# A folded Fourier layer: the end-token row moves from VectorE to TensorE, the weight splits become 1024 wide, and the modulation rows are handed out one per weight tile

## The chip, the cores and the metric

The kernel runs on one NeuronCore of one Trainium2 chip. The metric is the device time of one execution in microseconds; the figure for a kernel is the median of its timed runs. One further execution is taken by the hardware profiler, with a time of its own. The engines in the profile are PE (matmul), PEld (its weight load), DVE (VectorE), ACT (ScalarE) and SP, whose queue issues all the loads here; POOL is idle.

## The reference

Two layers over 256 latent tokens (`x`) and 256 context tokens (`ctx`) of width 2048, in float32. The even layer does retention (A) and Fourier mixing (B), the odd one a gated short convolution. Every layer is an adaLN-modulated RMSNorm first and a gated residual add last.

```python
shift, scale, gate = split(silu(c) @ ada_w[i] + ada_b[i], 3)      # per layer, also with c_ctx for ctx
hx = rmsnorm(x, norm_w[i]) * (1 + scale) + shift
# layer 0 (even): w_in is 2048 x 10240
qx, kx, vx, gax, ux, gbx = split(hx @ w_in);  qc, kc, vc, ... = split(hc @ w_in)
A = retention(qx, kx, vx | states of ctx) * silu(gax)
f = fft2(ux per group of 256 channels, over tokens and channels).real
B = (f @ fno_w per group) * silu(gbx)
x = x + gate * (concat(A, B) @ w_out)
# layer 1 (odd): w_in is 2048 x 16384
bg, cg, xt, g = split(h @ w_in);  y = bg * conv3(cg * xt) * silu(g)
x = x + gate * (y @ w_out)
return rmsnorm(x, final_norm_w)
```

The real part of the two-dimensional transform has a token symmetry: tokens t and 256-t enter only by their sum and their difference. So the kernel folds hx over the tokens (`fold_x`): 128 even columns (sums, t = 0..127) and 128 odd columns (differences). Column 0 of the sums holds tokens 0 and 128 added. Their difference goes in the place of the odd column 0, which has no use of its own there; it belongs to the even part of the channels. That is the end-token row, and it needs a projection of its own.

## The kernel before

**Splits.** Every weight tile is 128 x 2048 in float32, loaded by `load_raw` (line 83) from SP into a ring of three buffers, 1 MB each. `split_w` (line 88) cuts it into four pieces of 512 columns. Of each, ACT casts a rounded part `whi` (line 98) and DVE subtracts to get the rest `wlo` (`sub`, line 59). Both have rings of six. PE then multiplies `whi` by the activations, whose high and low parts lie side by side in 512 columns, and `wlo` by the high 256 columns alone. So one tile is 16 matmuls of 512 columns and 16 of 256 (`group_t`, line 123, PSUM tile `gT`). `group_n` (`gN`) does the same with the weights as the moving side, `group_d` (`gD`) in 256 columns. All matmuls have line 56.

**Order.** A scheduler that knows the program puts the instructions of each engine in a fixed order. Each engine then runs its own in that order and waits by semaphore. The program itself has two lists of side work. `hook()` takes one entry of `stages` after each half tile. `bg()`, called behind each tile's load, takes one of 64 `tasks`: a load of 1 MB of the modulation matrix (`raw<-adaT`, the same ring of three) and one pass of DVE over it (line 375, 128 x 2048). Row by row these make the gates of layer 0 and all the modulation of layer 1. While `quiet` is set, `bg()` does nothing; while `often` is set, it takes a task at every tile, and else at every second one. `finish_mods(first, last)` (line 762) does at once the rows below `last` that are still missing.

**Stages in time.** Prologue: modulation rows of layer 0 and the first projection, both bound to loads. Retention, four head pairs, with 28 tasks. In the last pair (quiet) `fold_x` makes the eight folded tiles `hf`, four of them during the queries' projection, three between heads, the last after the gates.

Then the Fourier part, still quiet: eight gate groups `gate_unfold` (line 724, two tiles each, from `hf`, the sigmoid's input unfolded by DVE), and beside the first four the 16 steps of `u0`, beside the last four the 16 steps of `u1` (class `half`, line 607). A step takes one 128-row block of the projection weights. `fold` adds and subtracts their halves on DVE (channels are folded too), two 512-wide splits follow, and six matmuls into `pu`. For the end-token row DVE also accumulates `uacc += weights * xd` (line 639), where `xd` is the end-token difference of hx; a matmul with `e0` puts the sum over partitions into row 0 of `pu` at the end. `u1`'s stages also run the Fourier matrices of groups 0 to 3 (`fourier`, line 660: `tables` with PSUM `pz`, `tokens` with `pP`, `product` with `py`, `gate`). Groups 4 to 7 run beside the first group of the output projection (`t_out`, line 757). `tables` loads its 256 KB (`wr`, line 675) itself. PSUM has three two-bank buffers (`pu`, `gT`, `gN`) and two one-bank buffers (all other names).

The output projection `w0o` (`project`, line 771) has eight blocks of four tiles. From block 6 on it is quiet. Line 756 has cleared `often`, so 12 tasks lie in its first six blocks. Behind it, `finish_mods(16, 48)` does eight rows in one go, then 16 `modulate` calls make `h1` for layer 1. Layer 1 is 16 blocks of eight tiles of `w1`, the first quiet, with the last 16 tasks behind it at every second tile; then eight blocks of `w1o`.

## Time and profile before

| | |
|---|---|
| three timed runs | 1850.09, 1849.87, 1865.33 us; median 1850.09 |
| the profiled execution | 1845.95 us, span 1844.1 us, mean granted PE clock 0.982 |
| PE / DVE / ACT busy | 1761.7 / 1271.0 / 895.6 us |
| loads | 397.03 MB read, 216 GB/s over the span |

A busy time counts an engine as busy while an instruction is in flight, and matmuls overlap, so a PE that shows as fully busy can still be slowed by its clock. The column PEclk tells that apart. The stages are read by a view that cuts the span into stretches and gives each engine's busy time in each, its clock and the loads' rate.

### The profile page before, as it was taken

The page shows a single profiled execution, that of the slowest core. Times are in us where ns is not written, and L with a number is a line of the kernel's source. Part 1 is how long each engine was busy: PE and PEld are TensorE (multiplying, and loading weights), DVE is VectorE, ACT ScalarE, POOL GpSimd, SP SyncE. Part 2 cuts the span into 40 slices and gives each one's busy share as a digit, 9 for nine tenths or more (in the row PEclk, how much of TensorE's full clock was granted, in tenths as well). Part 3 has the DMA queues.
Part 4 walks back from the last instruction along what each step waited for, and adds up shares of the span by engine and source line. Part 5 has one row for each costly group of instructions (what it writes and reads, how often), then busy time and mean ns, then how long its engine had stood idle before and what let it go on. Part 6 is the DMA issues. An engine that isn't in the chain of part 4 may idle for free.

```text
span 1844.1 us, 26501 instructions
## 1 busy us (share of the span) xinstructions
PE 1761.7 (96%) x10022; PEld 1506.7 (82%) x10022; DVE 1271.0 (69%) x2034; ACT 895.6 (49%) x1484; POOL 0.2 (0%) x4
## 2 busy tenths in 40 slices
PE   5999999999979997999969999999999999999997
PEld 3667888888858786888958888888888888888887
DVE  5448857756489996777687888666666666665554
ACT  4235625354445454445445555555555555555553
POOL 0000000000000000000000000000000000000000
PEclk9999999999989998999979999999999999999999
DMA  9886656652335554687666777555555555555552
GB/s 390 341 315 264 224 200 226 242 214 92 137 109 207 215 189 164 221 305 274 230 250 251 282 289 289 195 199 185 186 198 189 184 196 191 183 193 195 183 190 108
DMA packets 58737, 400.85 MB, mean 217 GB/s; under 512 B 6512, under 2 KB 6896, under 8 KB 11376
## 3 DMA queue, kind: packets, MB, share of 16 engines
q1 hardware_dynamic: 58608, 399.16, 59.2%
q8 instruction: 78, 1.28, 0.3%
q14 instruction: 51, 0.42, 0.1%
HBM read 397.03 MB, written 2.10 MB: 216 GB/s over the span
## 4 chain that ended last, share of the span: by engine, by line
PE 90%; DVE 4%; DMA 3%; ACT 1%; issue 1%; SPq 0%; DVEq 0%; ACTq 0%
PE gT L56 69%; PE gN L56 7%; PE gD L56 2%; PE gemv L56 2%; PE pu L56 2%; PE o L56 1%; DMA raw<-adaT 1%; PE pvx L56 1%; PE pk L56 1%; PE pvc L56 1%; DVE wlo L59 1%; DMA wr<-fno 1%; PE S L56 1%; PE pq L56 1%; DVE raw L375 1%
## 5 line engine op out<-in xcount | busy, mean ns | idle before, releaser
L59 DVE TENSOR_TENSOR wlo<-raw,whi 128x512 fp32r<-128x512 f32 x1056 | 714.7, 689 | 376.6 <-ACT whi L98 355.3
L98 ACT CAST whi<-raw 128x512 fp32r<-128x512 f32 x1024 | 626.8, 620 | 690.2 <-PE gT L56 512.1
L56 PE MATMUL gT<-h,whi 128*128 128x512 f32 x2048 | 712.6, 395 | 15.6 <-DVE h L202 15.0
L56 PE MATMUL gT<-h,wlo 128*128 128x256 f32 x2048 | 567.8, 278 | 0.0
L56 PEld LDWEIGHTS gT<-h,whi 128*128 128x128 f32 x2048 | 384.9, 188 | 105.4 <-issue 15.4
L56 PEld LDWEIGHTS gT<-h,wlo 128*128 128x128 f32 x2048 | 385.8, 188 | 0.4
L375 DVE CUSTOM_DVE_ANT_0 raw<-raw,scb 128x2048 f32<-128x2048 f32 x64 | 146.5, 2290 | 71.4 <-DMA raw<-adaT 68.2
L56 PE MATMUL gT<-hx,whi 128*128 128x512 f32 x448 | 161.6, 399 | 1.6 <-ACT v L493 1.6
L56 PE MATMUL gT<-y,whi 128*128 128x512 f32 x448 | 155.4, 394 | 0.0
L56 PE MATMUL gT<-hx,wlo 128*128 128x256 f32 x448 | 126.5, 282 | 0.0
L56 PE MATMUL gT<-y,wlo 128*128 128x256 f32 x448 | 124.1, 277 | 0.0
L56 PEld LDWEIGHTS gT<-hx,whi 128*128 128x128 f32 x448 | 83.9, 188 | 21.2 <-ACT v L493 2.1
L56 PEld LDWEIGHTS gT<-y,whi 128*128 128x128 f32 x448 | 84.0, 188 | 19.5
L56 PE MATMUL gT<-hf,whi 128*128 128x512 f32 x256 | 93.2, 400 | 1.7 <-ACT whi L98 1.7
L56 PEld LDWEIGHTS gT<-hx,wlo 128*128 128x128 f32 x448 | 84.6, 189 | 1.2 <-DVE wlo L59 0.5
L56 PEld LDWEIGHTS gT<-y,wlo 128*128 128x128 f32 x448 | 84.1, 188 | 0.0
L56 PE MATMUL gT<-yA,whi 128*128 128x512 f32 x224 | 80.4, 401 | 2.8 <-ACT whi L98 2.8
L56 PE MATMUL gT<-yB,whi 128*128 128x512 f32 x224 | 78.4, 394 | 0.2 <-ACT whi L98 0.2
L56 PE MATMUL gT<-hf,wlo 128*128 128x256 f32 x256 | 73.2, 286 | 0.3 <-DVE wlo L59 0.2
L185 ACT COPY lr_r<-gT 128x512 f32<-128x512 f32 x103 | 59.9, 581 | 7.3 <-PE gT L56 7.2
L56 PE MATMUL gT<-yA,wlo 128*128 128x256 f32 x224 | 63.0, 281 | 0.0
L56 PE MATMUL gT<-yB,wlo 128*128 128x256 f32 x224 | 62.1, 278 | 0.6 <-DVE wlo L59 0.6
(269 smaller groups left out, 2197.0 us busy)
## 6 DMA issues: line engine op xcount, KB each, us to landing
raw<-w SPq DMA_DIRECT2D x168, 1024.0 KB, 4.8
raw<-adaT SPq DMA_DIRECT2D x64, 1024.0 KB, 5.4
raw<-ada SPq DMA_DIRECT2D x32, 1024.0 KB, 7.0
raw<-w0o SPq DMA_DIRECT2D x32, 1024.0 KB, 4.9
raw<-w1o SPq DMA_DIRECT2D x32, 1024.0 KB, 4.8
raw<-w0g SPq DMA_DIRECT2D x16, 1024.0 KB, 4.8
raw<-w0u SPq DMA_DIRECT2D x16, 1024.0 KB, 4.8
raw<-w0s SPq DMA_DIRECT2D x8, 1024.0 KB, 5.7
```

What stands on the lines that cost most here:

```text
L56: nc.tensor.matmul(o, l, r, start=start, stop=stop, skip_group_check=True)
L59: nc.vector.tensor_tensor(o, x, hi.bitcast(F32), op=ALU.subtract)
L98: nc.scalar.copy(hi[:], sl)
L185: nc.scalar.copy(r[:], t[:, :, 256:512])
L375: nc.vector.tensor_tensor_reduce(out=raw[:], in0=raw[:], in1=scb[:], scale=1.0, scalar=0.0, op0=ALU.mult, op1=ALU.add, accum_out=gv[:, j:j ...
```

## The change

- **Splits 1024 wide.** `split_w` casts and subtracts 1024 columns at a time, with rings of three (the same memory). The first projection keeps 512 for the pieces that borrow other tiles.
- **End-token row on PE.** `xd` and `uacc` go. A tile `sd` holds the end-token column of `hf`, high and low, for each of the 16 blocks (`ends`). Each step adds two matmuls of 512 columns with 32 stationary columns into a bank `pd` that is held over the 16 steps. `finish` adds its two rows by a matmul with `e0` and copies them into row 0.
- **Steps.** A step folds its own 512 columns of weights (two DVE instructions of 512 instead of half of two of 1024) and splits sum and difference in one 1024-wide pair.
- **First gates from hx.** Gates 0 to 3 use the unfolded `hx`, with no unfolding after. Gates 4 to 7 stay on `hf`.
- **Folding later.** `fold_x` 0 to 2 stay in the last retention pair, one at a time; 3 to 7 run in the stages of `u0`, with kc = 0, 2, 4, 6, 8.
- **Fourier tables.** The 256 KB load is a stage of its own, some stages earlier, in a buffer of its own; its split takes a 1024-wide pair. The single-row operands of `tokens` are used where they lie, without four copies.
- **Modulation rows.** `often` stays set. The tasks behind the Fourier part come one per tile.

```diff
+        def wide():
+            return (wp.tile([P, 1024], F32R, tag="whi", bufs=3, name="whi"),
+                    wp.tile([P, 1024], F32R, tag="wlo", bufs=3, name="wlo"))
+        def part(pair, c0, n=512):
+            return pair[0][:, c0:c0 + n], pair[1][:, c0:c0 + n]
+        def cut(x, hi, lo):
+            nc.scalar.copy(hi, x)
+            sub(lo, x, hi)
         def split_w(raw, spare=None):
 
             parts = []
-            for pc in range(4):
-                sl = raw[:, pc * 512:(pc + 1) * 512]
-                if spare and pc == 3:
-                    hi, lo = spare()
+            for c0 in (0, 1024):
+                w = wide()
+                q = [part(w, 0), part(w, 512)]
+                if spare and c0:
+                    q[1] = tuple(t[:] for t in spare())
+                    for i in range(2):
+                        cut(raw[:, c0 + 512 * i:c0 + 512 * i + 512], *q[i])
                 else:
-                    hi = wp.tile([P, 512], F32R, tag="whi", bufs=6, name="whi")
-                    lo = wp.tile([P, 512], F32R, tag="wlo", bufs=6, name="wlo")
-                nc.scalar.copy(hi[:], sl)
-                sub(lo[:], sl, hi[:])
-                parts.append((hi, lo))
+                    cut(raw[:, c0:c0 + 1024], w[0][:], w[1][:])
+                parts += q
...
-        xd = const.tile([P, 16], F32, name="xd")
-
-        def fold_x(e):
-            s = rp.tile([P, 2, 256], F32, tag="t2", bufs=5, name="hs")
+        def fold_x(pool, e):
+            nb = 5 if pool is rp else 4
...
-                stages += [(lambda e=e: fold_x(e)) for e in range(4)]
+                stages += [None, lambda: fold_x(rp, 0), None, lambda: fold_x(rp, 1)]
                 q = queries()
                 h0, h1 = heads()
-                stages += [h0[0], lambda: fold_x(4), h0[1], lambda: fold_x(5), h0[2], h1[0], lambda: fold_x(6), h1[1]]
+                stages += [h0[0], None, h0[1], h1[0], h0[2], lambda: fold_x(rp, 2), h1[1], None]
...
-                fold_x(7)
...
+        sd = fp.tile([P, 16, 32], F32R, name="sd")
...
+        def ends(e):
+            nc.vector.tensor_copy(sd[:, 2 * e:2 * e + 2, 0:1], hf[e][:, :, 128:129].bitcast(F32))
+            nc.vector.tensor_copy(sd[:, 2 * e:2 * e + 2, 1:2], hf[e][:, :, 384:385].bitcast(F32))
+        for e in range(3):
+            ends(e)
...
+            def fold(self, kc):
+                if kc % 2 == 0:
+                    self.raw = load_raw(a["w0u"][self.hf * 8 + kc // 2])
+                r = self.raw[:].rearrange("p (k s c) -> p k s c", k=2, s=2)[:, kc % 2, :, :]
+                w = wide()
+                x = fp.tile([P, 1024], F32, tag="ef", name="ef")
+                add(x[:, 0:512], r[:, 0, :], r[:, 1, :])
+                dif(x[:, 512:1024], r[:, 0, :], r[:, 1, :])
+                cut(x[:], w[0][:], w[1][:])
+                self.w = part(w, 0), part(w, 512)
 
             def step(self, kc):
                 if self.pu is None:
-                    self.pu = psum("pu")
+                    self.pu, self.pd = psum("pu"), bank("pd")
                     self.fold(0)
-                i, k2 = kc // 2, kc % 2
-                ef, r = self.raws[i]
-                w = []
-                for src in (ef[:, k2, :], r[:, k2, 0, :]):
-                    hi = wp.tile([P, 512], F32R, tag="whi", bufs=6, name="whi")
-                    lo = wp.tile([P, 512], F32R, tag="wlo", bufs=6, name="wlo")
-                    nc.scalar.copy(hi[:], src)
-                    sub(lo[:], src, hi[:])
-                    w.append((hi[:], lo[:]))
-                if kc == 0:
-                    nc.vector.tensor_scalar(self.acc[:], r[:, k2, 1, :], xd[:, 0:1], None, op0=ALU.mult)
-                else:
-                    nc.vector.scalar_tensor_tensor(self.acc[:], r[:, k2, 1, :], xd[:, kc:kc + 1], self.acc[:],
-                                                   op0=ALU.mult, op1=ALU.add)
+                k2, w = kc % 2, self.w
                 x = hf[kc // 2]
                 for s in range(2):
                     c0 = s * 128
-                    mm3(self.pu[:, s, :], (x[:, k2, c0:c0 + 128], x[:, k2, 256 + c0:384 + c0]), w[s], kc == 0,
-                        kc == 15 and s == 0)
-                if k2 and i < 7:
-                    self.fold(i + 1)
-                if kc == 15:
-
-                    mm(self.pu[:, 1, :], e0[:], self.acc[:], False, True)
-                    self.h = fp.tile([P, 2, 512], F32R, tag="uh", name="uh")
-                    self.l = fp.tile([P, 2, 512], F32R, tag="ul", name="ul")
-                    nc.scalar.copy(self.h[:], self.pu[:])
-                    sub(self.l[:], self.pu[:], self.h[:])
-
-                    for t in (self.h, self.l):
-                        t0 = t[:, 1, :].rearrange("p (g c) -> p g c", g=4)[:, :, 0:1]
-                        nc.vector.tensor_scalar(t0, t0.bitcast(F32), row0[:], None, op0=ALU.mult)
+                    mm3(self.pu[:, s, :], (x[:, k2, c0:c0 + 128], x[:, k2, 256 + c0:384 + c0]), w[s], kc == 0, kc == 15)
+                mm(self.pd[0:32, :], sd[:, kc, :], w[0][0], kc == 0, False)
+                mm(self.pd[0:32, :], sd[:, kc, :], w[0][1], False, kc == 15)
+                if kc < 15:
+                    self.fold(kc + 1)
+                else:
+                    self.finish()
...
+                ds = fp.tile([P, 512], F32, tag="t2", bufs=4, name="ds")
+                nc.scalar.copy(ds[0:32, :], self.pd[0:32, :])
+                mm(self.pd[0:32, :], e0[0:32, :], ds[0:32, :], True, True)
+                h = self.h = fp.tile([P, 2, 512], F32R, tag="uh", name="uh")
+                l = self.l = fp.tile([P, 2, 512], F32R, tag="ul", name="ul")
+                p = self.pu
+                cut(p[:, 0, :], h[:, 0, :], l[:, 0, :])
+                nc.scalar.activation(h[:, 1, :], p[:, 1, :], AF.Copy, scale=rest[:])
+                nc.vector.scalar_tensor_tensor(l[:, 1, :], p[:, 1, :], rest[:], h[:, 1, :].bitcast(F32),
+                                               op0=ALU.mult, op1=ALU.subtract)
+                for t in (h, l):
+                    t0 = t[:, 1, :].rearrange("p (g c) -> p g c", g=4)[:, :, 0:1]
+                    nc.vector.tensor_copy(t0, zero4[:].unsqueeze(2))
+                cut(self.pd[0:1, :], h[0:1, 1, :], l[0:1, 1, :])
...
+            def load():
+                wr = got["wr"] = fp.tile([P, 512], F32, tag="wr", bufs=1, name="wr")
+                nc.sync.dma_start(wr[:], a["fno"][g].rearrange("p a c -> p (a c)"))
...
+        def gate_of(g):
+            tg, = group_t(a["w0g"], 2 * g, 2, [hx if g < 4 else hf])
             s = lr(fp, tg, bufs=4, ring=4)
+            sgb[g] = fp.tile([P, 2, 256], F32, tag="sgb", bufs=4, name="sgb")
+            if g < 4:
+                nc.scalar.activation(sgb[g][:], s[:], AF.Silu)
+                return
...
+        def folds(kc):
+            def f():
+                if kc % 2 == 0 and kc < 10:
+                    fold_x(fp, 3 + kc // 2)
+                    ends(3 + kc // 2)
+            return f
+        stages += [both(lambda kc=kc: u0.step(kc), folds(kc)) for kc in range(15)]
+        stages += [both(lambda: u0.step(15), gs[0][0])]
         for g in range(4):
-            gate_unfold(g)
-        stages += [both(lambda kc=kc: u1.step(kc), *((middle,) if kc == 0 else ()), gs[kc // 4][kc % 4])
+            gate_of(g)
+        stages += [both(lambda kc=kc: u1.step(kc), *((middle,) if kc == 0 else ()), gs[kc // 4][kc % 4 + 1],
+                        *((gs[kc // 4 + 1][0],) if kc % 4 == 1 else ()))
...
-        quiet[0] = often[0] = False
+        g5[0]()
+        g4[2]()
+        stages += [both(g4[3], g5[1], g6[0], g5[2]), both(g4[4], g5[3], g6[1], g7[0], g6[2]),
+                   both(g5[4], g6[3], g7[1], g7[2]), both(g6[4], g7[3]), g7[4]]
+        quiet[0] = False
```

The order on SP in the output projection `w0o`, some blocks into it (`adaT` are the tasks' loads, `xr` the residual's). Before:

```order
L85 DMA raw_7153<-w0o 128x2048
L85 DMA raw_7215<-w0o 128x2048
L85 DMA raw_7217<-adaT 128x2048
L85 DMA raw_7268<-w0o 128x2048
L85 DMA raw_7318<-w0o 128x2048
L85 DMA raw_7320<-adaT 128x2048
L813 DMA xr_7212<-xT 128x512
L85 DMA raw_7371<-w0o 128x2048
L85 DMA raw_7433<-w0o 128x2048
```

And now:

```order
L85 DMA raw_6304<-w0o 128x2048
L85 DMA raw_6306<-adaT 128x2048
L85 DMA raw_6361<-w0o 128x2048
L85 DMA raw_6363<-adaT 128x2048
L85 DMA raw_6406<-w0o 128x2048
L85 DMA raw_6408<-adaT 128x2048
L85 DMA raw_6451<-w0o 128x2048
L847 DMA xr_6358<-xT 128x512
L85 DMA raw_6453<-adaT 128x2048
L85 DMA raw_6496<-w0o 128x2048
```

Every `w0o` tile is now followed by an `adaT` load; before, every second one was.

The order on DVE from the last block of `w0o` to the first `modulate` of layer 1 (`ISA` is the pass over a modulation row, `x1_7` the last residual, `rstd` the norm, `mods` the finished modulation, `modt` and `h1` the two halves of `modulate`). Before, with four of the eight rows ahead of these:

```order
L775 SCALAR_TENSOR_TENSOR x1_7_6547<-gD_7862,mods_77,xr_7860 128x256 x2
L375 ISA raw_8154,gv_76<-raw_8154,scb_1185 128x2048
L375 ISA gv_76 128x1
L194 RECIPROCAL rstd_8139<-rstd_8139 128x256
L375 ISA raw_8157,gv_76<-raw_8157,scb_1185 128x2048
L375 ISA gv_76 128x1
L375 ISA raw_8160,gv_76<-raw_8160,scb_1185 128x2048
L375 ISA gv_76 128x1
L375 ISA raw_8163,gv_76<-raw_8163,scb_1185 128x2048
L375 ISA gv_76 128x1
L65 TENSOR_TENSOR mods_77<-gv_76,cols_70 128x32
L819 SCALAR_TENSOR_TENSOR mods_77<-mods_77,cols_70 128x16
```

And now:

```order
L59 TENSOR_TENSOR wlo_7294<-raw_7291,whi_7293 128x1024
L59 TENSOR_TENSOR wlo_7298<-raw_7291,whi_7297 128x1024
L59 TENSOR_TENSOR wlo_7442<-raw_7439,whi_7441 128x1024
L59 TENSOR_TENSOR wlo_7446<-raw_7439,whi_7445 128x1024
L809 SCALAR_TENSOR_TENSOR x1_7_5963<-gD_7116,mods_77,xr_7114 128x256 x2
L59 TENSOR_TENSOR wlo_7484<-raw_7481,whi_7483 128x1024
L206 RECIPROCAL rstd_7361<-rstd_7361 128x256
L212 SCALAR_TENSOR_TENSOR modt_7374<-x1_0_5956,mods_77,rstd_7361 128x256
L212 SCALAR_TENSOR_TENSOR modt_7378<-x1_0_5956,mods_77,rstd_7361 128x256
```

The passes and `mods` are gone from this place; splits of the first `w1` tiles (`raw_7439`, `raw_7481`) stand there instead.

The order on PE at the first step of `u0` (`hf0` is the first folded tile). Before:

```order
L56 MATMUL pu_4335<-whi_4342,hf0_3819 128x512 x2
L56 MATMUL pu_4335<-wlo_4343,hf0_3819 128x512
L56 MATMUL pu_4335<-whi_4346,hf0_3819 128x512 x2
L56 MATMUL gT_4300<-hf4_3999,whi_4395 128x512
L56 MATMUL pm_5090<-dmh_4293,hf0_3819 128x8 x2
L56 MATMUL pu_4335<-wlo_4347,hf0_3819 128x512
```

And now:

```order
L56 MATMUL pu_3919<-whi_3923,hf0_3522 128x512 x2
L56 MATMUL pd_3920<-whi_3923,sd_3868 32x512
L56 MATMUL pu_3919<-wlo_3924,hf0_3522 128x512
L56 MATMUL pu_3919<-whi_3923,hf0_3522 128x512 x2
L56 MATMUL pu_3919<-wlo_3924,hf0_3522 128x512
L56 MATMUL pd_3920<-wlo_3924,sd_3868 32x512
L56 MATMUL pu_3919<-whi_3938,hf0_3522 128x512 x2
L56 MATMUL pd_3920<-whi_3938,sd_3868 32x512
```

Each step has two more matmuls among its six, with 512 columns of weights moving and 32 stationary columns of `sd`.

More of the change, by code (lines that the diff above doesn't have):

```diff
@@ L557, in body @@
         ch, cl = table(a["dftc"], 512, "c")
-        e0 = fp.tile([P, P], F32, name="e0")
+        e0 = fp.tile([P, 32], F32, name="e0")
         nc.vector.memset(e0[:], 0.0)
         nc.vector.memset(e0[:, 0:1], 1.0)
-        row0 = fp.tile([P, 1], F32, name="row0")
-        nc.vector.memset(row0[:], 0.0)
-        nc.vector.memset(row0[0:1, :], 1.0)
-        mids = [fp.tile([P, 32], F32R, name=f"mid{i}") for i in range(4)]
-        zero = fp.tile([P, 32], F32, name="zero")
-        nc.vector.memset(zero[:], 0.0)
-        for t in mids:
-            nc.vector.tensor_copy(t[:], zero[:])
+        rest = fp.tile([P, 1], F32, name="rest")
+        nc.vector.memset(rest[:], 1.0)
+        nc.vector.memset(rest[0:1, :], 0.0)
+        sd = fp.tile([P, 16, 32], F32R, name="sd")
+        zero = fp.tile([P, 512], F32, tag="t2", bufs=4, name="zero")
+        nc.vector.memset(zero[:], 0.0)
+        nc.vector.tensor_copy(sd[:], zero[:].rearrange("p (k c) -> p k c", k=16))
+        def ends(e):
[3 more added lines that the diff above has]
+            ends(e)
         wm = fp.tile([P, 16, 2, 8], F32, tag="t2", bufs=4, name="wm")
@@ L671, in split_bank @@
                 return hi, lo
+            def load():
+                wr = got["wr"] = fp.tile([P, 512], F32, tag="wr", bufs=1, name="wr")
+                nc.sync.dma_start(wr[:], a["fno"][g].rearrange("p a c -> p (a c)"))
             def tables():
-                wr = fp.tile([P, 512], F32, tag="t2", bufs=4, name="wr")
-                nc.sync.dma_start(wr[:], a["fno"][g].rearrange("p a c -> p (a c)"))
-                wgh = wp.tile([P, 512], F32R, tag="whi", bufs=6, name="wgh")
-                wgl = wp.tile([P, 512], F32R, tag="wlo", bufs=6, name="wgl")
-                nc.scalar.copy(wgh[:], wr[:])
-                sub(wgl[:], wr[:], wgh[:])
+                wgh, wgl = part(wide(), 0)
+                cut(got["wr"][:], wgh, wgl)
                 pz = bank("pz")
@@ L731, in gate_unfold @@
             dif(n[:, :, 129:256], s[:, :, 127:0:-1], s[:, :, 255:128:-1])
-            sgb[g] = fp.tile([P, 2, 256], F32, tag="sgb", bufs=4, name="sgb")
             nc.scalar.activation(sgb[g][:], n[:], AF.Silu, scale=0.5)
```

57 lines of the change are left out of this document (23 added, 34 removed).

## The prediction

> **What bounds it now.** The head of the page and the table by stages come first; the stages are cut where PE's work changes.
>
> ```profile
> span 1844.1 us, 26501 instructions
> PE 1761.7 (96%) x10022; PEld 1506.7 (82%) x10022; DVE 1271.0 (69%) x2034; ACT 895.6 (49%) x1484; POOL 0.2 (0%) x4
> core 0: us, PE busy (x) PEld busy (x) DVE busy (x) ACT busy (x) POOL busy (x), PEclk, DMA share, GB/s
> 300.00:411.00 111.00, 110.99 (x567) 94.95 (x566) 76.58 (x105) 50.59 (x79) 0.00 (x0) 1.00 0.60 221
> 528.50:537.20 8.70, 0.67 (x2) 0.27 (x2) 8.43 (x24) 4.24 (x6) 0.00 (x0) 0.69 0.12 36
> 537.20:614.90 77.70, 73.79 (x373) 60.90 (x374) 73.48 (x113) 42.29 (x75) 0.00 (x0) 0.93 0.57 209
> 614.90:708.80 93.90, 88.13 (x502) 75.23 (x501) 86.08 (x156) 47.23 (x87) 0.00 (x0) 0.98 0.53 191
> 708.80:767.00 58.20, 48.35 (x297) 43.13 (x298) 36.81 (x68) 23.92 (x42) 0.00 (x0) 0.91 0.46 163
> 767.00:896.80 129.80, 129.80 (x750) 113.47 (x749) 93.23 (x136) 64.83 (x107) 0.00 (x0) 1.00 0.74 274
> 920.00:939.00 19.00, 1.91 (x9) 1.01 (x7) 17.97 (x24) 5.68 (x12) 0.00 (x0) 0.61 0.95 363
> 953.40:1808.00 854.60, 854.60 (x4932) 747.34 (x4931) 578.74 (x902) 444.64 (x740) 0.00 (x0) 1.00 0.59 210
> ```
>
> PE never stops from 767 to 897 or from 953 to 1808, and not in retention (the row from 300 to 411). What a narrower or wider split saves on DVE there is worth nothing. PE loses time in four stretches that the change touches: the seam at 528, the two halves of the Fourier part (where DVE is busy for 73.5 of 77.7 and 86.1 of 93.9 us), the Fourier tail at 709, and the seam between the layers at 920. So the sum has two sides: what these give back, and what the added PE work and the added loads cost where PE is full.
>
> PE's prices come from the chain of waits, each a stretch without a gap:
>
> ```profile
> 584.24 2.31 PE pu L56 x10
> 622.42 1.19 PE pz L56 x10
> 946.67 861.51 PE gT L56 x4968
> ```
>
> A 512-column matmul of a step takes 0.231 us, a 256-column one of the Fourier matrices 0.119, a projection matmul 0.1734 on average, so a tile of 32 takes 5.55 us.
>
> **Fourier part, added PE work.** 32 steps with two more matmuls of 512 columns: 64 x 0.231 = 14.8 us. Only 32 stationary columns are used, but the trace gives no reason for less: streaming 512 columns is what the row above shows. The two `e0` matmuls stay. PE's own need by stages, in full-clock time:
> - u0 (537 to 615): 96 step matmuls 22.2, seven gate tiles 38.9, about 1 for `e0`, and before 5.7 for the 48 short `pm` matmuls (priced like the `pz` row). Before 68, now 69.5 (the `pm` go, 7.4 come).
> - u1 (615 to 709): 22.2, eight tiles 44.4, four groups of 37 matmuls 17.6, `e0` 1. Before 85, now 98 (5.7 and 7.4 come).
> - tail (709 to 767): four tiles 22.2, four groups 17.6, a rest of 1.4. 41 both times.
>
> Before 194 of 229.8 us, so 36 are waiting and slow clock. Now 208.5.
>
> **Fourier part, DVE.**
>
> ```profile
> L59 DVE TENSOR_TENSOR wlo<-raw,whi 128x512 fp32r<-128x512 f32 x1056 | 714.7, 689 | 376.6 <-ACT whi L98 355.3 <-PE gT L56 6.3 <-issue 0.3
> L639 DVE SCALAR_TENSOR_TENSOR uacc<-raw,xd,uacc 128x512 f32<-128x512 f32 x30 | 22.4, 745 | 0.0
> L65 DVE TENSOR_TENSOR ef<-raw 128x1024 f32<-128x1024 f32 x16 | 19.5, 1217 | 0.0
> L59 DVE TENSOR_TENSOR ul<-pu,uh 128x1024 fp32r<-128x1024 f32 x2 | 2.4, 1220 | 0.0
> L653 ACT CAST uh<-pu 128x1024 fp32r<-128x1024 f32 x2 | 2.0, 1012 | 3.9 <-PE pu L56 3.9
> L65 DVE TENSOR_TENSOR hs<-hx 128x512 f32<-128x512 f32 x8 | 5.5, 684 | 0.0
> L68 DVE TENSOR_TENSOR eo<-hs 128x254 f32<-128x254 f32 x8 | 3.3, 417 | 0.0
> L65 DVE TENSOR_TENSOR un<-t 128x256 f32<-128x256 f32 x8 | 3.4, 420 | 0.1
> ```
>
> A step before: half of two 1024-wide instructions 1.22, two splits 1.38, `uacc` 0.745: 3.35. Now two of 512 (1.38) and one split of 1024 (1.22): 2.60. A tile's splits fall from 4 x 0.689 = 2.76 to 2 x 1.22 = 2.44. So u1 loses 16 x 0.75 + 8 x 0.32 = 14.6 of its 86 us, and PE, at 98, becomes its bound. u0 loses 12 + 2.2 in steps and tiles and four unfoldings (two instructions of 0.42 each and a small one), but takes over five foldings of about 2.3 (two of 0.68, two of 0.42, small ones): it ends near 67, below PE's 69.5.
>
> In u0, DVE has most of this extra work at the start: the order puts the zeroing of `sd`, the tables and the foldings 3 and 4 ahead of the second gate tile's splits. PE gets steps 0 to 2 in that time, 5.5 us of work, and its clock is low there anyway after the seam. I add the 6 us that half clock for 12 us costs, as before: u0 takes 76 (bounds 70 and 82; before 77.7). u1 gets 3 us of waits, 101 (98 and 108; before 93.9): `pd` holds one of the two one-bank buffers for all 16 steps, so `pz`, `pP` and `py` take turns in the other.
>
> The tail's 17 us of waiting are these:
>
> ```profile
> PE pz L56 <- ACT wgh L678: 11.8, 4, 6.1
> 709.43 4.70 DMA wr<-fno
> 717.99 4.69 DMA raw<-adaT
> 725.51 6.32 DMA wr<-fno
> ```
>
> The 256 KB `wr` loads stood on SP behind weight and `adaT` loads, and PE waited 6.1 us for one split. They are issued a group earlier now. But four `adaT` loads instead of two lie in this stage, ahead of `wr` on SP, and their passes are ahead of the splits in DVE's fixed order. I take half of the 17: the tail is 49 (bounds 41 and 58). At the seam, folding 7 leaves DVE's path and a longer first split comes: 1 us (0 to 2) gained. Together 229.8 - (76 + 101 + 49) + 1 = **5 us gained** (bounds 22 gained, 18 lost).
>
> **Between the layers.**
>
> ```profile
> 919.01 0.40 PE L56 MATMUL gD<-yB,whi 128*128 128x256 f32 x2
> 921.85 0.87 DVE L775 SCALAR_TENSOR_TENSOR x<-gD,mods,xr 128x256 f32<-128x256 f32 x2
> 925.58 1.75 DVE L194 RECIPROCAL rstd<-rstd 128x256 f32<-128x256 f32 x1
> 927.24 2.23 DVE L375 CUSTOM_DVE_ANT_0 raw<-raw,scb 128x2048 f32<-128x2048 f32 x1
> 934.75 1.28 DVE L200 SCALAR_TENSOR_TENSOR modt<-x,mods,rstd 128x256 f32<-128x256 f32 x3
> 938.98 0.76 PE L56 MATMUL gT<-h,whi 128*128 128x512 f32 x1 [15.02 <-DVE h L202]
> ```
>
> Three passes lie between `rstd` and the first `modt`, and the first splits of `w1` behind them. Without them `modt` starts at `rstd`'s end. That itself comes about 1.7 earlier: PE ended near 920, and the residual `x` stood behind another pass until 921.85. So `modt` starts at 927.3 - 1.7 = 925.6 in place of 934.75: 9.2 us. Fewer splits stand among the `modulate` calls (the first tile's are done): another 3. **12 us gained** (9 to 14). What is late next is DVE's rate of `h1`, about 1 us for a block that PE uses in 0.69.
>
> **The rows that moved.** The 24 tiles of `w0o` blocks 0 to 5 now carry 24 `adaT` loads for 12; the four of block 0 are in the tail above. In the other 20, a block of four tiles moves 8 x 1.0486 MB + 0.26 MB = 8.65 MB in 22.2 us: 390 GB/s.
>
> ```profile
> 20.00:60.00 40.00, 33.90 (x209) 22.77 (x205) 20.42 (x38) 14.56 (x25) 0.00 (x0) 0.91 0.97 391
> raw<-adaT SPq DMA_DIRECT2D x64, 1024.0 KB, 5.4
> raw<-w0o SPq DMA_DIRECT2D x32, 1024.0 KB, 4.9
> L375 DVE CUSTOM_DVE_ANT_0 raw<-raw,scb 128x2048 f32<-128x2048 f32 x64 | 146.5, 2290 | 71.4 <-DMA raw<-adaT 68.2 <-ACT scb L370 2.7
> 917.00 6.22 DMA raw<-adaT
> ```
>
> The prologue reaches 391 at a share of 0.97, with more buffers. So the loads would run at their limit. [...]
>
> The ring of three binds about as tightly. A weight tile holds its buffer while it lands and until the second half's split: landing plus about 3.4 (one cast and two splits). A task holds it for landing plus 2.3. Two landings and 5.7, over three buffers, is 5.4 us a tile with 4.9 and 5.4 as landings, which fits into 5.55. With 6.2, as in the burst of tasks, it is 6.0. I take 5.85 for 20 tiles: **6 us lost** (0 to 9). DVE's sum there is 2.44 + 2.29 + about 0.6 for the residual's share = 5.3 of 5.55, with little to spare for a wait. The last 12 tasks lie on 12 adjoining tiles of `w1` for 16 spread over 32: **3 lost** (0 to 6).
>
> **Wider splits where PE is full.** Two halves in reserve behind the running one are 5.55 us of cover, of which a cast (1.01) and a split (1.22) take 2.2. DVE may then stand still for 3.3 us; with six pieces it was about 5.6.
>
> ```profile
> DVE raw L375 <- DMA raw<-adaT: 68.2, 37, 5.8
> ```
>
> DVE waits up to 5.8 us for a task's load, mostly in retention, where PE has matmuls of its own between (`o`, `S`) and two-stream tiles of twice the length. I put **1 us** (0 to 6). Casts and subtractions elsewhere hide behind PE as they did: nothing.
>
> **Sum.** 5 + 12 - 6 - 3 - 1 = 7 us gained. The profiled execution took 1845.95 us and would take 1839; the timed median is 4 us higher, 1850.09, so I predict **1843**.
>
> **Rivals.**
> - *The loads hide and PE alone bounds the Fourier part.* u0 72, u1 98, tail 43, seam 1 give 18; between the layers 12; the rest costs 2. Gain 28: 1822. For it: DVE drops below PE in both halves. Against it: 390 GB/s.
> - *Ring-bound rows* (the slower side). If both landings are 6.2 and a pass waits 1 us in DVE's queue, a tile takes (2 x 6.2 + 5.7 + 1) / 3 = 6.4, and 32 tiles (20 and 12) lose 27 us. With 5 + 12 - 1 gained: 1861; with a tail that stays at 58, 1870. It decides from 0.5 us a tile, where the gains are used up. For it: the burst's 6.22. Against it: dense tasks in retention, where PE did not stop.
> - *The one free bank.* If PE stands still 1.5 us at each of the 12 handovers among `pz`, `pP` and `py`, u1 takes 116 and the whole 1858. Against it: the order puts 10 to 30 other matmuls between most of them.
>
> **Chances.** Forecast 0.53, first rival 0.22, ring 0.15, bank 0.10. 1% is 18.5 us, about what a measurement of this kernel can tell (its three runs spread by 15). Below 1831.6 lie most of the first rival and a little of the forecast: 0.23. Above 1868.6 the worse half of the ring's case and a rest: 0.09. The range takes in all but the far ends of both: 1823 to 1863.
>
> **What would show it.** The order between the layers: `modt` right behind `rstd`, and no gap of PE over 5 us there. PE's clock at 1.00 and DVE below PE in u1, whose length is 98 to 104. In `w0o`, waits of DVE's passes for `adaT` and of PE for `wlo`; none of the latter means that the 6 us are not lost. `pz` no longer waits 6 us for its split. The forecast is wrong if PE has gaps in layer 1 behind the last task, or if retention has them at all.

## The result, and the profile after

The changed kernel takes 1865.46 us (median of 20 runs, 1843.21 to 1872.93), the one before 1848.83 (20 runs). The medians are 16.6 us apart. The ratio is 1.0063, 95% interval 1.0038 to 1.0089: about 12 us lost where 7 were forecast to be gained. That is inside the 1% that the prediction set as its limit, and on the other side of zero; the median lies 2.5 us above the top of the range, 1863. The ratio goes by the fast runs, which leave out two of the kernel after above 1872 us, the profiled execution among them, though its granted clock of 0.984 is that of other runs too.

The profiled execution took 1872.29 us, 7 above the median. Head of the page and the table by stages, cut as before where PE's work changes:

```profile
span 1870.4 us, 24593 instructions
...
PE 1803.3 (96%) x10086; PEld 1524.3 (81%) x10086; DVE 1192.3 (64%) x1465; ACT 804.3 (43%) x955; POOL 0.2 (0%) x4
core 0: us, PE busy (x) PEld busy (x) DVE busy (x) ACT busy (x) POOL busy (x), PEclk, DMA share, GB/s
300.00:411.00 111.00, 111.00 (x569) 95.20 (x568) 76.84 (x83) 46.80 (x54) 0.00 (x0) 1.00 0.61 230
...
540.80:628.20 87.40, 82.99 (x385) 63.04 (x385) 77.19 (x129) 43.90 (x53) 0.00 (x0) 0.92 0.55 200
628.20:728.40 100.20, 100.11 (x572) 83.78 (x571) 75.74 (x98) 46.11 (x61) 0.00 (x0) 0.97 0.51 187
728.40:783.00 54.60, 49.95 (x312) 43.89 (x312) 38.92 (x49) 21.36 (x29) 0.00 (x0) 0.94 0.56 207
783.00:913.00 130.00, 126.76 (x715) 108.99 (x714) 103.46 (x106) 52.30 (x57) 0.00 (x0) 1.00 0.89 339
...
1060.00:1830.00 770.00, 769.62 (x4357) 667.10 (x4356) 445.14 (x495) 339.94 (x380) 0.00 (x0) 1.00 0.53 188
```

DVE fell from 1271 to 1192 us of work and stands below PE in every row, as the change meant. But PE's own busy time rose by 41.6 us, and the 64 added matmuls explain 14.8 of them, at 0.231 us each. The last row is the odd one: from 1060 on PE is busy for 769.62 of 770 us at clock 1.00, and yet layer 1 takes longer than before. The same 200 us in the middle of it, before and after:

```profile
1400.00:1600.00 200.00, 200.00 (x1156) 174.90 (x1155) 130.65 (x211) 102.71 (x170) 0.00 (x0) 1.00 0.54 190
```

```profile
1400.00:1600.00 200.00, 200.00 (x1134) 173.42 (x1133) 117.34 (x131) 87.82 (x100) 0.00 (x0) 1.00 0.54 188
```

PE is full in both and gets 1156 matmuls done in one and 1134 in the other, 1.9% fewer. The timeline of PE, before and then after, shows how (start, duration, engine, line, what; `x1` is one matmul):

```profile
1400.00 0.39 PE L56 MATMUL gT<-h,whi 128*128 128x512 f32 x1
1400.23 0.27 PE L56 MATMUL gT<-h,wlo 128*128 128x256 f32 x1
1400.34 0.40 PE L56 MATMUL gT<-h,whi 128*128 128x512 f32 x1
1400.58 0.28 PE L56 MATMUL gT<-h,wlo 128*128 128x256 f32 x1
1400.69 0.39 PE L56 MATMUL gT<-h,whi 128*128 128x512 f32 x1
```

```profile
1400.07 0.40 PE L56 MATMUL gT<-h,whi 128*128 128x512 f32 x1
1400.31 0.28 PE L56 MATMUL gT<-h,wlo 128*128 128x256 f32 x1
1400.43 0.40 PE L56 MATMUL gT<-h,whi 128*128 128x512 f32 x1
1400.66 0.28 PE L56 MATMUL gT<-h,wlo 128*128 128x256 f32 x1
1400.78 0.40 PE L56 MATMUL gT<-h,whi 128*128 128x512 f32 x1
1401.01 0.28 PE L56 MATMUL gT<-h,wlo 128*128 128x256 f32 x1
1401.12 0.40 PE L56 MATMUL gT<-h,whi 128*128 128x512 f32 x1
```

Before, a pair of 512 and 256 columns follows the last one after 0.343 and 0.350 us by turns, 0.3467 on average. After, three pairs make a cycle of 0.361, 0.349 and 0.350: 0.3533. No engine is waited for in either. Below, these are called the fast and the slow *pace*. In both traces both paces occur (before has 0.3532 from 477 to 498 us, the kernel after 0.3467 from 306 to 338); what differs is which of them PE keeps in layer 1.

The gap between the layers went as forecast (rows of before: `modt` at 934.75, a gap of 15.02):

```profile
939.88 1.75 DVE L206 RECIPROCAL rstd<-rstd 128x256 f32<-128x256 f32 x1 [0.79 <-ACT rstd L205]
941.67 1.28 DVE L212 SCALAR_TENSOR_TENSOR modt<-x,mods,rstd 128x256 f32<-128x256 f32 x3
943.49 0.67 PE L56 MATMUL gT<-h,whi 128*128 128x512 f32 x1 [4.15 <-DVE h L214]
```

By the starts of PE's matmuls the two executions, and four of the experiments below, divide like this (us; `ss` is the sum of squares behind the last head, and each half ends with the second of its `e0` matmuls; the last row is part of the others: the sum over all pairs of what each took above 0.3466):

```
stage                            before   after  a_pace36 an_pace36 b_tail36 best_pace
start to last ss of retention     528.8   532.4     529.5     528.2    529.5     529.3
seam, to the first pu               8.4     8.4       8.4       8.7      8.4       8.4
u0, to its last e0                 77.0    87.2      87.2      84.7     73.1      74.1
u1, to its last e0                 94.0    99.8      99.8     101.5     88.0      88.1
tail and w0o, to the last gD      211.4   208.8     205.8     204.0    197.9     206.6
to the first gT of layer 1         19.4     6.9       6.9       6.6     20.3       6.6
w1                                713.6   732.4     720.0     717.7    714.0     717.3
w1o, to the last gD               178.3   181.3     178.3     178.3    178.3     178.3
of this, slow pace                  2.5    19.1       7.2       8.0      2.6       7.4
```

Of the 26 us between the first two columns 16.6 are pace, 16.1 were lost in u0 and u1, and 12.5 came back between the layers. Without the pace, retention takes 3 us more, `w1` 6.8 more, and tail and `w0o` 3.6 less.

### The profile page after: what moved, and what is told of

Same layout as the page of the kernel before. It is cut to its first block, busy times and chain, and to the rows that moved or that the text cites. A ratio compares the mean times of both kernels' runs of the same rounds, so it can differ in the third digit from the quotient of the medians.

```text
span 1870.4 us, 24593 instructions
## 1 busy us (share of the span) xinstructions
PE 1803.3 (96%) x10086; PEld 1524.3 (81%) x10086; DVE 1192.3 (64%) x1465; ACT 804.3 (43%) x955; POOL 0.2 (0%) x4
## 4 chain that ended last, share of the span: by engine, by line
PE 84%; DVE 6%; DMA 5%; issue 2%; ACT 2%; SPq 0%; DVEq 0%; ACTq 0%
PE gT L56 61%; PE gN L56 7%; PE gD L56 2%; DMA raw<-w0o 2%; PE gemv L56 2%; DMA raw<-adaT 2%; DVE wlo L59 2%; PE pu L56 2%; PE o L56 1%; PE pk L56 1%; PE pvx L56 1%; PE pvc L56 1%; DVE raw L387 1%; ACT whi L97 1%; PE S L56 1%
## 5 line engine op out<-in xcount | busy, mean ns | idle before, releaser
L59 DVE TENSOR_TENSOR wlo<-raw,whi 128x1024 fp32r<-128x1024 f32 x520 | 623.3, 1206 | 489.4 <-ACT whi L97 488.2
L97 ACT CAST whi<-raw 128x1024 fp32r<-128x1024 f32 x520 | 534.7, 1036 | 807.4 <-PE gT L56 527.7
L56 PE MATMUL gT<-h,whi 128*128 128x512 f32 x2048 | 724.4, 399 | 4.5 <-DVE h L214 4.2
L56 PE MATMUL gT<-h,wlo 128*128 128x256 f32 x2048 | 576.1, 281 | 5.0 <-DVE wlo L59 4.9
L56 PE MATMUL gT<-hx,whi 128*128 128x512 f32 x576 | 210.4, 403 | 2.5 <-ACT v L504 2.5
L56 PE MATMUL gT<-hx,wlo 128*128 128x256 f32 x576 | 163.2, 283 | 0.0
L56 PEld LDWEIGHTS gT<-hx,whi 128*128 128x128 f32 x576 | 109.3, 190 | 29.8 <-ACT v L504 2.9
L56 PEld LDWEIGHTS gT<-hx,wlo 128*128 128x128 f32 x576 | 109.9, 191 | 2.8 <-DVE wlo L59 0.5
L56 PE MATMUL gN<-whi,hx 128*128 128x512 f32 x192 | 59.7, 392 | 0.0
L56 PE MATMUL gN<-whi,hc 128*128 128x512 f32 x192 | 59.5, 390 | 0.0
```

The source lines that it names most:

```text
L56: nc.tensor.matmul(o, l, r, start=start, stop=stop, skip_group_check=True)
L59: nc.vector.tensor_tensor(o, x, hi.bitcast(F32), op=ALU.subtract)
L97: nc.scalar.copy(hi, x)
```

## The experiments

**Is it the wider splits?** Since both the width and the pace were new in layer 1, the first pair put the width alone on the kernel before, and took it alone from the kernel after.

```diff
 b_wide (on before)
-            for pc in range(4):
-                hi = wp.tile([P, 512], F32R, tag="whi", bufs=6, name="whi")
+            for c0 in (0, 1024):
+                w = wide()     # 1024 wide, rings of three
 a_narrow (on after): the reverse, in fold() and tables() too
```

> The kernel before with one edit: weight tiles are split 1024 columns at a time from rings of three, everything else as before. Theory A (the wide splits slow the whole of PE's steady work): a 512+256 pair of matmuls in the projections takes 0.353 us in the profile in place of 0.347, and the kernel takes some 15 to 17 us longer than before, near 1865. Theory B (the width costs what the prediction's sum says, and the slower pace of the profile after belongs to that execution alone): 0 to 3 us longer, pairs at 0.347.

> The kernel after with one edit: splits 512 wide from rings of six, as before the change. Theory A: the pairs are back at 0.347 us and the time falls by 15 to 17 us, to about 1848, as the loss in the Fourier half and the gain between the layers are left. Theory B: the time stays within 3 us of the kernel after.

b_wide: 1852.77 us (ratio 1.0037, 1.0002 to 1.0072); a_narrow: 1853.29 (1.0011, 0.9988 to 1.0035). The medians agree with neither theory, and the profiles contradict both: b_wide had the fast pace in layer 1 (44.37 us a block) but the slow one in `w0o` (22.6 a block for 22.2), and a_narrow had the slow one in layer 1 (45.22) with 512-wide splits. So the width does not make the pace. The single runs of a_narrow lie in two groups, 1841 to 1846 and 1853 to 1858. In b_wide's profile the width costs little else in all: its span is 3.6 us longer than before's, and 3.4 of that is slow pace. (u1 is 7.4 longer in it, and tail and `w0o` without the pace 4.7 shorter. In the Fourier steps b_wide keeps two cuts of 512, in the halves of one wide pair.)

**The other parts alone.** Two more took one part each from the kernel after.

```diff
 a_rows
-        quiet[0] = False
+        quiet[0] = often[0] = False
 a_fold
-                stages += [None, lambda: fold_x(rp, 0), None, lambda: fold_x(rp, 1)]
+                stages += [(lambda e=e: fold_x(rp, e)) for e in range(4)]
 (and 4 to 7 in the same pair, none in u0; all gates from hf)
```

> The kernel after with one edit: the modulation rows after the Fourier part are again taken with every second tile, as before the change, so 7 blocks of w0o hold about 10 rows in place of 20 and the rest are read later. If the rows' density costs what the marks of the two traces say (w0o blocks longer by 14 us in all from the first to the last, 11 to 12 us gained between the layers), the two nearly cancel: within 3 us of the kernel after. If the density is the costly part (ring-bound rows), it is faster than the kernel after by more than 5 us.

> The kernel after with one edit: all eight foldings of hx stand in the last retention pair again and all gates are made from folded hx and unfolded, as before the change. If the ten us that the u0 stage lost (76.5 to 86.8 us) come from the five foldings that VectorE now does there, the stage is at 76 to 79 us and the time 8 to 10 us below the kernel after. If they come from each step's fold, cast and subtraction one after the other through single buffers, the stage stays above 84 us.

a_rows: 1853.42 us (1.0036, 1.0012 to 1.0061), a_fold: 1865.26 (1.0086, 1.0053 to 1.0119). Both profiles had the slow pace in layer 1 (22.2 and 20.2 us of it in all), so the marks have to be read. By its median a_rows is 12 us below the kernel after, as its second expectation had it, but nine of its runs lie at 1849 to 1855 and three near 1866, so that pace and rows are mixed in it. Without the slow pace, tail and `w0o` took 197.3 in place of 207.4 in a_rows and `w1` 713.1 in place of 720.3, and the gap was 18.9 in place of 6.9. So the dense rows cost 10.1 + 7.2 and gain 12.0: 5 us lost, with wide splits. In a_fold u0, to its last `e0`, took 81.6 for 87.2: the later foldings cost 5.6 us there, between the two expectations, and the median did not show it.

The six profiles by then hold 60 uninterrupted runs of 20 pairs or more: 21 were fast and 37 slow from their first pairs to their end, but for the last pairs of one. That one (at 807.8 us) and two more (at 839.4 and 885.8), all in `w0o` of the kernel after, went over from slow to fast without a gap between matmuls. There a weight load (PEld) came late behind a `wlo` split, by 0.01, 0.08 and 0.04 us. In all other such pairs in the traces of both kernels this load starts with the matmul of `whi`, 0.005 us behind it at most. The case at 839.4:

```profile
838.20 2.36 DVE L59 TENSOR_TENSOR wlo<-raw,whi 128x1024 fp32r<-128x1024 f32 x2 [1.21 <-ACT whi L97]
839.40 0.40 PE L56 MATMUL gT<-yB,whi 128*128 128x512 f32 x1
839.48 0.19 PEld L56 LDWEIGHTS gT<-yB,wlo 128*128 128x128 f32 x1
839.63 0.28 PE L56 MATMUL gT<-yB,wlo 128*128 128x256 f32 x1
```

Layer 1 holds one run of over 700 us, which 1.9% makes 14 us. Which pace it gets looked like a matter of where in PE's cycle the last wait ended.

**Entering the stream on purpose.** To test that, PE's phase was shifted by an extra matmul that nobody needs.

```diff
 pace_map (on a_narrow, ahead of each group from block 3 of layer 1; n = 16 to 416)
+            mm(bank("dum")[:, 0:n], streams[0][0][:, 0, 0:128], streams[0][0][:, 0, 0:n], True, True)
 pace_map2 (from block 4; n = 16 to 476, two adjoining groups each)
+            if fst and n:
+                mm(ps[0][:, 0, 0:n], hi[:, 0:128], streams[0][0][:, 0, 0:n], True, False)
```

> The kernel after with 512-wide splits, and with one extra matmul of 16 to 416 columns (each of 26 widths twice, in mixed order) ahead of each of the 52 projection groups of layer 1 from block 3 on; it writes a bank that nobody reads. In the profiles so far PE keeps one of two paces, 0.3467 or 0.3533 us for a pair of 512 and 256 columns, from one interruption of its stream of pairs to the next, and a stretch of 700 us without an interruption keeps the pace in which it began. Theory C (the pace is a matter of the phase at which the stream is entered, not of the widths or of what VectorE and ScalarE do): the pace changes from group to group here, within one profile, with the extra matmul as the only difference; both paces are seen, and a group keeps its own for all its 32 pairs. Theory D (the pace is a property of the execution or of the kernel's work on the other engines): all groups from block 3 on show the same pace, 45.2 us a block, as in the profile of the kernel after.

> As the run with extra matmuls ahead of the groups of layer 1, but each is now a first matmul of its group done twice (with 16 to 476 columns, into the same bank, which the real one then starts anew), so that it stays at its place. From block 4 on, 24 widths follow one another, each in two adjoining groups. Theory C (the phase at the entry sets the pace): the pace of a group follows from the width of the extra matmul and the pace before it; some widths lead to 0.3467 us, others to 0.3533, and no group changes its pace without an interruption. Theory D (the paces come by chance, or from other engines): no order in the widths, and changes inside groups.

In pace_map the instruction order drew 48 of the 52 extra matmuls forward, ahead of 1058 us. The other four stood at their groups, and behind them the pace was 0.3467 (400 columns), 0.3532 (160), 0.3466 (416) and 0.3534 (336), the last up to the end of the kernel. pace_map2 holds the order. What stood ahead of a group, and what followed (f fast, s slow):

```
columns   36   56   76   136  156 | 16   116  376  400 | 96   176  196  216  416
1st      s>f  f>f  f>f  s>f  f>f | ?>s  s>s  s>s  s>s | f>f  f>s  f>f  s>f  s>f
2nd      f>f  f>f  f>f  f>f  f>f | s>s  s>s  s>s  s>s | f>s  s>f  f>s  f>s  f>s
```

Of the ten widths not shown, 296 and 436 led to the fast pace, 236, 276, 356, 456 and 476 to the slow one, and 256, 316 and 336 to both. No group changed its pace within its 32 pairs once its first pairs were through. With the other engines' work the same throughout, the pace changes where PE enters the stream anew, and with the width at the entry. That is theory C, and D is refuted. But width and pace ahead don't settle it alone: 96 columns led from the fast pace to both. That it matters at which pair of the cycle an entry falls is a guess of mine, and no run shows it.

**The pace as cause of the time.** Six such matmuls, at the start of blocks 4 to 9 of layer 1, with widths picked from that list.

```diff
+            if b == 4:
+                turns += [n for w in WIDTHS for n in (w, 0, 0, 0)]
 a_pace, b_pace: (36, 136, 56, 76, 156, 56)      b_slow: (16, 376, 400, 16, 376, 400)
```

> The kernel before with the same six extra matmuls. Theory C: the runs of before near 1864 go, the others stay: 1845 to 1851, and the kernel after with its pace set is slower than this by 2 to 8 us, which is what the change costs by itself. Theory D: as before, with some runs near 1864.

> The kernel before with six extra matmuls at the same places, on 16, 376 and 400 columns twice over: the widths after which the pace was 0.3533 us. Theory C: blocks of 45.2 us in layer 1 from block 10 at the latest, and 13 to 16 us more than before, 1860 to 1866, from six matmuls that take 1 us together. Theory D: 1 us more than before.

> The kernel after with six first matmuls done twice, on 36 to 156 columns, at the start of blocks 4 to 9 of layer 1: the widths after which the pace was 0.3467 us in the run before, whatever it was ahead of them (0.11 us each). Theory C (the phase at which PE enters the stream sets the pace, and the change only led to an entry of the slow kind): the runs no longer spread over 1843 to 1873, they lie 14 us below the bulk of the kernel after, at 1849 to 1858, with blocks of 44.4 us from 1300 on. Theory D (the other engines' wider instructions hold PE back): no change, 1860 to 1873.

b_pace: 1848.96 us (0.9994, 0.9975 to 1.0014), all 12 runs between 1844.21 and 1853.5. b_slow: 1861.8 (1.0064, 1.0041 to 1.0087), all 8 runs between 1860.61 and 1864.71. The two programs differ in the columns of six matmuls. The same 200 us of b_slow and of b_pace:

```profile
1400.00:1600.00 200.00, 200.00 (x1133) 173.33 (x1132) 125.89 (x200) 101.14 (x168) 0.00 (x0) 1.00 0.53 188
```

```profile
1400.00:1600.00 200.00, 200.00 (x1156) 176.34 (x1155) 130.65 (x210) 103.05 (x170) 0.00 (x0) 1.00 0.54 191
```

x1133 is within one of the kernel after's row, and x1156 is that of before. So the pace is worth the 13 us by itself, on a kernel without any part of the change. That a few runs of the kernel before lie at 1860 to 1865, where b_slow lies, would have the same cause; no profile was taken of one.

a_pace: 1857.22 (1.0044, 1.0015 to 1.0072). In its profile 36 columns led to the fast pace, but 136, tried second, led from there to the slow one, where it had been fast with narrow splits, and the other widths did not lead out again. In b_pace 76 columns led to the slow pace for one block, and in b_slow the first 16 left the fast one as it was. The list holds for one kernel's timing only, and not strictly there.

**The change without the pace, and the width without the pace.** With 36 columns at all six places:

> The kernel after with first matmuls done twice on 36 columns only, at the start of blocks 4 to 9 of layer 1 (36 led to the fast pace in the profile of the run before). If the loss is mostly the pace: 1848 to 1854, all runs without those near 1867, at most 5 us above the kernel before. If the change's own work is the larger part: 1856 to 1860.

> The same with 512-wide splits in place of 1024. If the width costs nothing by itself: within 3 us of the run with 36 columns and wide splits. If it costs what the marks say (3 us in u0, 5 in w0o under dense rows, 3 to 6 under the tasks of layer 1): 8 to 12 us below it, 1840 to 1844.

a_pace36: 1855.64 us (1.0038, 1.0019 to 1.0056); an_pace36: 1844.72 (0.9972, 0.9951 to 0.9993); before beside them 1848.54. Both profiles have the fast pace from 1125 on. So of the 16.6 us between the medians 9.8 (1865.46 - 1855.64) go with the slow pace. The other 7.1 (against before beside it) are the change's own. The width alone is worth 10.9 (1855.64 - 1844.72): with 512-wide splits the change is 3.8 us *faster* than before. The expectation for the width was 8 to 12.

Where do 10.9 us lie, if layer 1 doesn't hold them? PE's waits between 945 and 1125, where the last 12 tasks run, in the kernel after and in an_pace36:

```profile
PE gT L56 <- DVE wlo L59: 4.9, 9, 0.8
```

```profile
PE gT L56 <- DVE wlo L59: 0.4, 2, 0.2
PE gT L56 <- ACT whi L94: 0.2, 1, 0.2
```

And the chain of waits there, of the kernel after and of an_pace36 (start, us, what):

```profile
1022.02 7.02 DMA raw<-adaT
1029.06 2.29 DVE raw L387
1031.39 7.09 DMA raw<-w
1038.57 1.06 ACT whi L97
...
1040.80 0.24 DVE wlo L59
```

```profile
1020.05 6.04 DMA raw<-w
...
1026.19 0.63 ACT whi L94
...
1026.85 0.70 DVE wlo L59
...
1027.60 32.43 PE gT L56 x180
```

Behind a tile that comes late, PE's first matmuls stand behind a cast and a split of the whole half: 1.06 + 1.22 us, where 0.63 + 0.70 did. Each pair of pieces is held longer too: for 16 matmuls, where a narrow one is for eight (2.8 and 1.4 us, an estimate from 5.55 a tile of 32). The wide kernel stays on its loads (`raw<-adaT`, task, `raw<-w`), the narrow one is back on PE at 1027.6. Averaged over the profiles of the kernel after and its versions with wide splits (three) and with narrow ones (four, and for `w1` the two that have no extra matmul in every group), and without the slow pace, the wide ones need 2.6 us more up to the end of retention, 2.2 in u0, 2.4 in tail and `w0o` and 4.3 in `w1`: 11.5, about what the runs say. The first of these is no larger than the spread among the three wide ones (527.8 to 530.6). That the latency of the first piece is the mechanism is argued from these rows; no run separated it from the longer hold of the buffers. And the width costs in layer 1 only together with the dense rows: with wide splits and rows at every second tile, `w1` without its slow pace takes 713.8 us in b_wide and 713.1 in a_rows, for 713.4 in before.

**u0, and the parts that gain.**

```diff
 a_nopd
+                if kc == 15:
                     mm(self.pd[0:32, :], sd[:, kc, :], w[0][0], ...)
 b_dense (on before)
-        quiet[0] = often[0] = False
+        quiet[0] = False
```

> The kernel after without 30 of the 32 pairs of matmuls that the end-token row added in each half (the sums for slices 0 to 14 of that row are left out). If PE bounds both halves, u0 and u1 are each 6.9 us shorter (86.8 to 80, 99.8 to 93). If u0 waits for VectorE's foldings and splits, u0 stays within 2 us of 86.8 while u1 falls to 93.

> The kernel before with one edit: after the Fourier part a modulation row is taken with every weight tile, not every second one. By the marks of the profiles so far the wait between the layers falls from 15 to 4 us and layer 1 carries fewer rows, while w0o grows by 5 to 10 us with 512-wide splits: 3 to 9 us shorter in all if PE keeps the fast pace in layer 1 (1839 to 1845), and 16 us above that if it falls into the slow one. If the rows are bound by the three load buffers, w0o grows by over 15 us and the time is not below that of before.

a_nopd (one run): u0 to its first `e0` 83.6 for 86.8, u1 from there to its own 93.4 for 99.8. 6.9 us of matmuls went from each. u1 gave 6.4 of that, u0 3.2: u1 is bound by PE, u0 only in part. u0's largest wait, in the kernel after and in a_nopd:

```profile
PE pu L56 <- ACT whi L97: 11.6, 4, 8.0
```

```profile
PE pu L56 <- ACT whi L97: 12.7, 5, 8.0
```

8.0 of each is the seam itself; the rest are casts that a step waits for. That these come late because fold, cast and split follow one another behind `fold_x` on DVE is read from the program's order, and not shown by itself.

b_dense: 1854.9 us (0.9996, 0.9962 to 1.003), its runs again in two groups, 1836 to 1842 and 1852 to 1859. In its profile (fast pace) the gap is 6.6 for 19.4, tail and `w0o` 215.5 for 211.4, `w1` 714.4 for 713.6: 12.8 gained, 4.9 lost (3.2 of it without the slow pace). u0 took 2.8 more, ahead of the rows. By this profile the dense rows gain as forecast with narrow splits, or better. The median does not show it: eight of the 12 runs lie in the upper group, some 16 us higher, where the slow pace would put them; none of those was profiled.

**Together.** On before: dense rows, the tail's new order with the `fno` loads a group earlier, the first gates from `hx`, single middle columns, and six extra matmuls for the pace; without the end-token row on PE, the later foldings and the wide splits. b_tail36 leaves out the dense rows and has 36 columns at all six places.

> The parts of the change that gained by the profiles, on the kernel before: a modulation row with every tile after the Fourier part, the fno tables loaded a group earlier with the new order of the tail, the first four gates from unfolded hx, the middle columns as single columns; but the end-token row on VectorE, the foldings in the last retention pair and 512-wide splits as before, and the six extra matmuls that set the pace. From the marks: 12 us gained between the layers, 8 to 10 in the tail, 3 to 5 lost in w0o: 1829 to 1836, faster than both kernels. If the tail's gain came from the end-token row on PE, 1838 to 1842.

> The fastest version without the denser rows: before, with the fno tables loaded a group earlier and the tail's new order, first four gates from unfolded hx, middle columns as single columns, end-token row on VectorE, 36 columns at the six places. If the Fourier part's gain is independent of the rows: 8 to 10 us in u0 and u1 and 9 in the tail stay, 1829 to 1833, and the denser rows are worth 8 more. If the rows hid there, 1838 or more.

best_pace: 1822.29 us (0.9858, 0.9819 to 0.9897). b_tail36: 1825.2 (0.9872, 0.9842 to 0.9902). Both are faster than the two kernels, and than expected: u0 and u1 together fell from 170.9 us to 162.2 and 161.0, tail and `w0o` (b_tail36) by 13.6. The rows of before had part of it: PE's 11.8 us of waiting in `pz <- ACT wgh` lie in u1 (614 to 708, the first row) as well as in the tail (708 to 770), and are gone.

```profile
PE pz L56 <- ACT wgh L678: 5.7, 3, 3.3
```

```profile
PE pz L56 <- ACT wgh L678: 6.1, 1, 6.1
```

What the other parts gave, the gates from `hx` in u0 for one, was not measured apart. DVE is still busy for 95 and 98% of the two halves in best_pace:

```profile
537.70:617.40 79.70, 77.02 (x401) 64.67 (x402) 75.94 (x112) 45.56 (x81) 0.00 (x0) 0.94 0.63 221
617.40:699.90 82.50, 80.98 (x478) 69.85 (x476) 80.79 (x127) 46.37 (x84) 0.00 (x0) 1.00 0.60 209
```

The dense rows, worth 13.8 us between the layers here, give 8.7 back in tail and `w0o` and 3.3 in `w1`, and 4.8 of these 12 us are slow pace; by the times 2.9 remain, which the two intervals do not tell from nothing. Against an_pace36, which has narrow splits, dense rows and the fast pace too, best_pace is 22.4 us faster, and u0 and u1 hold all of that (162.2 for 186.2). That is the price of the end-token row on PE with its later foldings and single-step folds: 5.6 are the foldings by a_fold, some 10 PE's added matmuls by a_nopd, and the rest was not separated.

## Why the prediction was wrong

1. **"A projection matmul 0.1734 on average, so a tile of 32 takes 5.55 us"**, and "casts and subtractions elsewhere hide behind PE as they did: nothing". This step failed first. PE was full in layer 1, and I took that for a fixed price. It has two: 5.55 and 5.65 us a tile. By pace_map2, which one holds hangs on where the stream was last entered, and a change ahead of it can draw anew. In the profiled execution it cost 16.6 us, in the median 9.8. The sum had no term for it; before's trace had both prices in retention, and I looked at averages.
2. **Wider splits where PE is full, 1 us (0 to 6).** Mis-sized: 10.9. Cover by two reserve halves is the right picture only while tiles arrive early. At the prologue, u0 and the tiles among the tasks they don't, and the first half's cast and split of 2.28 us for 1.33 stand in PE's way each time; so the rows argue. The sum priced width and dense rows apart, and they cost most together.
3. **u0 and u1: 177 forecast, 187.0 measured**, against 170.9 before (171.6 in the prediction's stretches). PE's work was 170.8 for the 167.5 that I had summed, since u0 has eight gate tiles, not seven. DVE's relief made PE the bound in u1, as said, and it took 99.8 for 101. u0 took 87.2 for 76, and this is the second step that failed: there the foldings ahead of the first steps cost 5.6, where the prediction let PE's own steps cover them, the width 2.2, and half clock for 13.6 us (PEclk 0.92) about 7 for the 6 put in. Some 2 us stay open.
4. **Tail 9 gained**: 8.9, read at the same work. From u1's last `e0` to the third block of `w0o`, by when both kernels have done the same matmuls, before takes 77.6 us and after 68.7. The `pz` wait went as forecast; waits for `whi` stayed (4.2 us for 3.1). The earlier loads were worth more than this step saw, since their lateness stalled u1 too (5.7 us there).
5. **Between the layers 12 gained**: 12.5. Right, step by step: `modt` stands right behind `rstd`.
6. **Rows in `w0o` 6 lost, in `w1` 3 lost**: blocks 1 to 5 of `w0o` took 118.8 for 112.6, 6.2 lost, and `w1` without the slow pace 6.8. Both sizes hang on the width: taken away alone, the dense rows are worth 10.1 (the tail included) and 7.2 with wide splits, and 2.6 and 0.6 with narrow ones (b_dense), all without the slow pace. 339 GB/s at a share of 0.89 is what the loads reached.
7. **Seam 1 gained**: 8.4 us in both. Nothing.

Without width and pace the sum was 8 us gained, and 3.8 were measured (an_pace36), which is partly luck: u0 and u1 lost 15.2 us there for the 5.4 forecast, and tail and `w0o` gained 8.5 for 3. The measured time came near the *ring-bound* rival's 1861, but not by its sum: the rows cost 13 us (6.2 + 6.8) for its 27, and pace and u0 did the rest. Part of its mechanism is there with wide splits: loads of 7 us each stand on the chain at 1022 and 1031. *One free bank* falls with u1 at 99.8 and no wait for `pz`; *PE alone bounds* with u0 and the tail. The sign the prediction named for itself, gaps of PE in layer 1, would not have found the loss: PE has none, and is slower.

## What to carry to other kernels

Where PE is full for hundreds of microseconds, count matmuls per 100 us in both traces before explaining anything else, since a busy share of 100% hid two paces here (1156 and 1134 matmuls in the same 200 us). What stood ahead of the stream flipped the pace (pace_map2), and six extra matmuls made layer 1 fast or slow by their widths alone (1848.96 us in b_pace, 1861.8 in b_slow). Widen the pieces of a split only where the tiles come early, since by the rows here the first piece's latency is paid at each late one (2.28 us for 1.33); on the kernel before, with its sparser loads, the width cost next to nothing apart from the pace. An engine that is busy for most of a stage need not bound it: earlier loads of eight small tables, with the lighter gates and single columns around them, gained 24 us (b_tail36 against b_pace; of this the waits for the tables were at most 11.8) while VectorE stayed as busy (95 and 98% of the two halves in best_pace, 95 and 92% before), and moving VectorE's row to PE, with what went with it, lost 22.

## What was not expected of the hardware

A stream of f32 matmul pairs, 512 and 256 columns with a new stationary tile each, ran at 0.3467 or 0.3533 us a pair in these profiles, in cycles of two or three pairs, for as long as nothing interrupted it (2439 pairs in 846 us before, 2174 in 768 us after). A weight load that came late by 0.08 us, by 0.04 or by 0.01 was interruption enough, with no gap between the matmuls. The granted clock was 1.00 in both, and the weight loads of layer 1 took 188 and 189 ns (`gT<-h,wlo`). In pace_map2 the pace was set at the entry: it changed there, and in no group once its first pairs were through. The streams in the other order, where the activations are stationary (`gN`), and the narrow last block (`gD`) kept one pace in both kernels' traces (0.227 us a matmul of 512 columns and 0.120 of 256). What holds the one or the other pace, and why a given width leads to it, stays open.
